# Output products of six heads as seven block products instead of eight, with one product copied by ScalarE into a second PSUM bank

## The chip, the cores and the metric

The kernel runs on one core of one Trainium2 chip. The metric is device time in microseconds (us) of one execution, the median of three runs. Five engines work side by side, each through its own instructions in order: PE (matrix products, with PEld for its weight loads), DVE (VectorE), ACT (ScalarE), POOL (GpSimd) and SP, which here only issues DMAs. They meet through semaphores. Matrix products are written to PSUM, which has eight banks of 128 partitions x 512 float32.

## The reference

A trunk of two layers is applied with the same weights to two groups of 512 tokens of width 1024. Each layer is `x = x + mixer(rms_norm(x))`. Layer 0 mixes by differential attention, layer 1 by retention in both directions; both have 8 heads of width 256 (`D_INNER` = 2048), a gate, and one output projection of 2048 x 1024:

```
o = rms_norm(o, subln_g, SUBLN_EPS) * (1.0 - lambda_init)     # layer 1: without the factor
o = o.reshape(B, S, D_INNER) * jax.nn.silu(gate)
return o @ w_out
```

A final RMS norm closes the trunk. What the change touches is `o @ w_out`: each head's 512 x 256 output times its 256 x 1024 rows of `w_out`, added to x.

## The kernel before, in words

Everything is float32 to the caller. A product of two float32 operands is done in three passes on operands split into a high and a low part (`PASSES`): high x high, high x low, low x high. `hi_of` (an ACT copy that rounds, line 481) makes the high part and `lo_of` (a DVE subtraction, line 484) the low one, so that every operand that is made costs both engines one instruction.

The program has four stages in time: projections of layer 0 (to about 620 us), attention with its output products (to about 1030), projections of layer 1 (to about 1480), and retention with its output products (to the end). The projections already use block products in seven multiplications (`P1` to `P7`, classes `Unit`, `Duo`, `WideDuo`); the output products do not.

Attention goes by `tiles` (head h, group g, 128 tokens t), two per turn of the loop: `scores`, `row_max`, `exps`, `combine`, `transp`, and after each second tile `av`, whose result `weigh` multiplies by the gate (`og`, line 1191) and splits into `oT`, and squares for the norm (lines 1195 and 1196). `weighed` gets the norm's factor `rr` (transposes on PE, sums on ACT, a power on POOL, line 1211). Retention goes by `blocks` (h, g), with `scores_both`, `states`, `av2` (c = 0, 1: 256 tokens each), `weigh`, and `weighed_both` (POOL lines 1911 and 1912 make `rr`).

Output products are owed (`owe`) as steps in a list `todo` that `fill` takes from while later tiles are worked on. A step (`out_step`) is one block of 128 tokens x 512 columns: six matmuls of 512 columns (two halves e of the head's 256 rows x three passes) into one of three `pj` banks of PSUM (line 1279), and then one DVE instruction (`axpy`, line 1284) that multiplies the bank by `rr` and adds it to x in SBUF. For 256 tokens of one head that is 4 steps, 24 matmuls and 4 axpys. The head's weights are loaded as two pieces of 128 x 1024 and each is split at that width (`out_weights`).

The order of instructions on each engine isn't written by hand. `Plan` records operations with costs and dependences, lists them by due time, and `SHIFTS` moves the due times of some operations by seeded random amounts; PE may take an operation up to 24 places early (`WINDOW`). What comes out is fixed when the program is built.

## Time and profile before

| | us |
|---|---|
| median of 3 runs | 1782.05 (1781.91 to 1782.11) |
| the profiled execution, its own time | 1782.33 |
| its span from first to last instruction | 1780.2 |
| PE busy | 1769.7 |
| DVE busy | 1550.6 |
| ACT busy | 926.9 |
| POOL busy | 118.5 |

An engine's busy time is the time in which one of its instructions was under way. Instructions of one engine overlap at their ends, so the step from one start to the next is shorter than an instruction's own duration; the step is what an instruction costs an engine that has no gaps.

### The profile page before, as it was taken

What the parts mean: (1) busy time and instruction counts of PE and PEld (TensorE: products, weight loads), DVE (VectorE), ACT (ScalarE), POOL (GpSimd) and SP (SyncE); (2) the same over time, 40 slices, a digit from 0 to 9 for tenths busy, and PEclk for the clock granted to TensorE, in tenths of its full rate; (3) what the DMA queues carried; (4) which work ended last, traced back from release to release, by engine and by line L of the source; (5) the groups of instructions that cost most, each with busy time, mean ns of one, the idle gap of its engine ahead of it and who ended that gap; (6) DMA issues with size and microseconds to landing.
All of it is one profiled execution on the core that took longest, in us unless ns stands there. A gap on an engine that the chain in (4) does not pass through costs nothing.

```text
span 1780.2 us, 28644 instructions
## 1 busy us (share of the span) xinstructions
PE 1769.7 (99%) x10485; PEld 1565.0 (88%) x10485; DVE 1550.6 (87%) x2660; ACT 926.9 (52%) x1947; POOL 118.5 (7%) x256
## 2 busy tenths in 40 slices
PE   9999999999999999999999999999999999999998
PEld 7889988888998888888888888899889988988887
DVE  8979779999979888888888898887998797888887
ACT  8664434544544565455455876444544455444446
POOL 1000000000000011111111100000000001111114
PEclk9999999999999999999999999999999999999999
DMA  6345535555555695455453624464565579665562
GB/s 233 102 153 168 177 118 160 171 160 168 190 175 155 218 332 187 174 189 190 168 190 105 213 77 155 138 200 166 172 206 179 176 222 407 236 232 194 217 221 95
DMA packets 162819, 328.85 MB, mean 185 GB/s; under 512 B 12772, under 2 KB 76920, under 8 KB 162680
## 3 DMA queue, kind: packets, MB, share of 16 engines
q1 hardware_dynamic: 162352, 326.71, 54.6%
q8 instruction: 82, 1.34, 0.3%
q14 instruction: 57, 0.47, 0.1%
q10 hardware_dynamic: 328, 0.34, 0.1%
HBM read 209.55 MB, written 117.44 MB: 184 GB/s over the span
## 4 chain that ended last, share of the span: by engine, by line
PE 98%; ACT 1%; DMA 1%; DVE 0%; issue 0%; POOL 0%; SPq 0%; POOLq 0%; DVEq 0%; ACTq 0%
PE pj L756 21%; PE pj L1279 19%; PE sc L756 11%; PE pj L766 10%; PE o L756 6%; PE o L1607 5%; PE sc L1546 5%; PE sc L766 5%; PE o L905 3%; PE o L991 2%; PE o L1864 1%; PE tp L1843 1%; PE sc L1816 1%; PE sc L1864 1%; PE pj L1587 1%; PE tp L1587 1%
## 5 line engine op out<-in xcount | busy, mean ns | idle before, releaser
L1279 PE MATMUL pj<-ws,arena 128*128 128x512 f32 (+1 forms) x1334 | 344.8, 390 | 0.0
L1279 PEld LDWEIGHTS pj<-ws,arena 128*128 128x128 f32 x1334 | 247.7, 188 | 50.4
L756 PE MATMUL pj<-b,ws 128*128 128x512 f32 x1080 | 263.5, 390 | 0.0
L481 ACT CAST ws<-st 128x512 fp32r<-128x512 f32 x264 | 161.1, 622 | 162.3 <-PE sc L756 37.5
L756 PEld LDWEIGHTS pj<-b,ws 128*128 128x128 f32 x1080 | 200.0, 188 | 40.4 <-issue 0.3
L484 DVE TENSOR_TENSOR ws<-st,ws 128x512 fp32r<-128x512 f32 x264 | 178.3, 687 | 50.8 <-ACT ws L481 38.4
L1284 DVE SCALAR_TENSOR_TENSOR b<-pj,pad,b 128x512 f32<-128x512 f32 (+1 forms) x257 | 189.6, 745 | 29.8 <-PE pj L1279 16.9
L756 PE MATMUL sc<-arena,ws 128*128 128x512 f32 x768 | 186.0, 390 | 0.0
L756 PEld LDWEIGHTS sc<-arena,ws 128*128 128x128 f32 x768 | 142.7, 188 | 28.9
L756 PE MATMUL pj<-arena,ws 128*128 128x512 f32 x636 | 156.0, 390 | 0.0
L756 PEld LDWEIGHTS pj<-arena,ws 128*128 128x128 f32 x636 | 118.8, 188 | 24.6 <-DVE ws L484 0.2
L481 ACT CAST ws<-raw 128x512 fp32r<-128x512 f32 (+2 forms) x140 | 103.2, 741 | 63.4 <-PE o L905 15.5
L484 DVE TENSOR_TENSOR ws<-raw,ws 128x512 fp32r<-128x512 f32 (+2 forms) x135 | 109.2, 813 | 23.4 <-ACT ws L481 21.1
L1564 ACT ACTIVATE b<-sc,pad 128x512 f32<-128x512 f32 x128 | 87.5, 691 | 74.3 <-DVE pad L1554 74.1
L766 PE MATMUL pj<-ws,b 128*128 128x256 f32 x960 | 116.1, 275 | 0.0
L766 PEld LDWEIGHTS pj<-ws,b 128*128 128x128 f32 x960 | 112.5, 188 | 0.3
L756 PE MATMUL o<-arena,ws 128*128 128x512 f32 x456 | 108.3, 390 | 0.4 <-DVE b L544 0.4
L1546 PE MATMUL sc<-arena 128*128 128x512 f32 x384 | 101.8, 398 | 0.7 <-ACT b L1564 0.7
L809 ACT COPY c<-pj 128x512 f32<-128x512 f32 x96 | 56.3, 588 | 87.1 <-PE pj L756 64.2
L756 PEld LDWEIGHTS o<-arena,ws 128*128 128x128 f32 x456 | 85.3, 188 | 18.3 <-DVE b L544 0.6
L481 ACT CAST os<-e 128x512 fp32r<-128x512 f32 x88 | 54.8, 622 | 77.6 <-DVE e L817 29.2
L1607 PEld LDWEIGHTS o<-arena 128*128 128x128 f32 x768 | 93.0, 188 | 2.4
(307 smaller groups left out, 3233.8 us busy)
## 6 DMA issues: line engine op xcount, KB each, us to landing
qk<-os SPq DMA_DIRECT2D x192, 256.0 KB, 3.6
arena<-qk SPq DMA_DIRECT2D x96, 512.0 KB, 7.0
v<-os SPq DMA_DIRECT2D x64, 512.0 KB, 3.6
arena<-v SPq DMA_DIRECT2D x64, 512.0 KB, 4.1
raw<-in_da_w_in_dram SPq DMA_DIRECT2D x51, 512.0 KB, 5.6
raw<-in_ret_w_in_dram SPq DMA_DIRECT2D x38, 512.0 KB, 5.0
os<-g SPq DMA_DIRECT2D x32, 512.0 KB, 7.2
g<-e SPq DMA_DIRECT2D x48, 256.0 KB, 4.2
```

The lines of the kernel that those rows point to most:

```text
L481: act(n, lambda: nc.scalar.copy(dst(), src()), r, w)
L484: dve(n, lambda: nc.vector.tensor_tensor(dst(), src(), hi().bitcast(F32), op=ALU.subtract), r, w)
L756: nc.tensor.matmul(ps.t, a[u][0]()[:, k, :], bt[k][:, v, :], start=(opens and k == 0 and i == 0), stop=(k == 3 and i == 2), skip_group_che ...
L766: nc.tensor.matmul(ps[:, (t % 2) * 256:(t % 2) * 256 + 256], bt[k][:, v, t * P:(t + 1) * P], a[u][0]()[:, k, :], start=(opens and t % 2 == ...
L809: act(S, lambda c=c, ps=ps: nc.scalar.copy(c.t, ps.t), [ps], [c])
L905: nc.tensor.matmul(ps[:, c0:c0 + 256], w[:, lo:lo + P], of(b, j), start=(start and j == 0 and i == 0), stop=(j == 1 and i == 2), skip_grou ...
L991: nc.tensor.matmul(ps[:, t * 256:t * 256 + 256], of(b, j, t), w[:, a, j], start=(start and t == 0 and j == 0 and i == 0), stop=(j == 1 and ...
L1279: nc.tensor.matmul(ps[:, here], o[a][:, e, t * P:(t + 1) * P], u[b][:, e, here], start=(m == 0), stop=(m == 5))
L1284: axpy(n, lambda half=half, here=here, ps=ps: nc.vector.scalar_tensor_tensor(half, ps[:, here], rr[:, t % 2:t % 2 + 1], half, op0=ALU.mult ...
L1546: nc.tensor.matmul(s.t, q[:, a, t * P:(t + 1) * P], k[:, b, :], start=(n == 0), stop=(n == 2))
L1564: act(840, lambda j=j, s=s, m=m: nc.scalar.activation(p[:, j, :], s.t, AF.Exp, bias=m.t, accum_out=sm[:, 2 * j + n:2 * j + n + 1]), [s, m] ...
L1607: nc.tensor.matmul(o[:, e * 256:(e + 1) * 256], v[b][:, j, e * P:(e + 1) * P], aT[a][:, j, :], start=(n == 0), stop=(n % 12 == 11), skip_g ...
```

## The change

For three heads of each layer (`FAST`: heads 2, 4, 6 of attention and 1, 3, 5 of retention), both groups and both halves c of the tokens, the product of a 256 x 256 block of o (2 x 2 blocks of 128) with the head's 256 x 1024 weights (2 x 2 blocks of 128 x 512) is done in seven block products instead of eight. Each is three matmuls. The seven share three `pj` banks: P1 goes to bank x, ACT copies x to bank y, P2 is added to y, P5 goes to z, P6, P7 and P4 are added to x and P3 to z. After P2, P5, P6, P7, P3 and P4 the bank is multiplied by `rr` and added to its quarter of x (`added`), six times in all.

Four sums of blocks of o are made per (h, g, c) on POOL (`block_sums`, 128 columns each) and split by ACT and DVE; the addition of the two halves of the squares moves from DVE to POOL for these heads. Per head four differences of weight blocks are made on POOL (512 columns each), and five operands of 512 columns are split (t1, t2, t3, t4, b22) beside one piece of 1024, where before two pieces of 1024 were. The first such product of a head issues the split of t4. `SHIFTS` has other and more entries (120 instead of 45).

```diff
+FAST = (2, 4, 6,), (1, 3, 5,)
...
 SHIFTS = (
-    (635.39, 16, 2, 0.05, 454008), (1473.67, 30, 2, 0.2, 912168), (1473.67, 8, 2, 0.2, 596270),
+    (1602.39, 8, 4, 0.5, 513480), (638.03, 16, 1, 0.5, 679689), (616.01, 30, 1, 1, 109496),
...
+        if dt == F32R and tag in ("e", "c", "m", "raw") or (tag, i) in rounded:
+            if rounded.get((tag, i), F32) != dt:
+                cnt[0] += 1
+                label = f"{tag}_{i}_{cnt[0]}"
+                places[tag, i] = pool.tile([P, size], dt, tag=f"{tag}{i}", name=label, bufs=1)
+            rounded[tag, i] = dt
...
+    def either(on, n, out, a, b, op, r, w):
+        plan.op(on, 0.2+0.0036*n if on == "POOL" else 0.07 + 0.00104 * n, lambda: (
+            nc.gpsimd if on == "POOL" else nc.vector).tensor_tensor(out(), a(), b(), op=op), r, w)
+    def block_sums(og, new):
+        x, hi, lo = st_t([P, S], "sums"), *(n(dt=F32R) for n in new)
+        a11, a21, a12, a22 = ((lambda k=k: og[:, k * P:(k + 1) * P]) for k in range(4))
+        s1, s2, s3, s4 = ((lambda k=k: x[:, k * P:(k + 1) * P]) for k in range(4))
+        for k, (o, a, b, fn, r) in enumerate((
+                (s1, a21, a22, ALU.add, [og]), (s2, s1, a11, ALU.subtract, [og, (x, 0)]),
+                (s3, a11, a21, ALU.subtract, [og]), (s4, a12, s2, ALU.subtract, [og, (x, 1)]))):
+            either('POOL', P, o, a, b, fn, r, [(x, k)])
+        hi_of(S, lambda: hi.t, lambda: x.t, [x], [hi])
+        lo_of(S, lambda: lo.t, lambda: x.t, lambda: hi.t, [x, hi], [lo])
+        return hi, lo
+    def weigh(y, sg, oT, c, scale=1.0, sq=None, sums=None, new=None):
         here = slice(c * 256, (c + 1) * 256)
-        og, sq = c_t("og"), sq or m_t("sq")
+        og, sq = e_t("og") if new and new[0] is m_t else c_t("og"), sq or m_t("sq")
         wide = lambda t: t.rearrange("p (e n) -> p e n", e=2)
         dve(S, lambda: nc.vector.tensor_tensor(wide(og.t), wide(y.t), sg[:, :, here], op=ALU.mult), [y, sg], [og])
         hi_of(S, lambda: oT[0][:, :, here], lambda: wide(og.t), [og], [(oT[0], c)])
         lo_of(S, lambda: oT[1][:, :, here], lambda: wide(og.t), lambda: oT[0][:, :, here], [og, (oT[0], c)],
               [(oT[1], c)])
         act(S, lambda: nc.scalar.activation(sq.t, y.t, AF.Square, scale=scale), [y], [sq])
-        dve(256, lambda: nc.vector.tensor_tensor(sq[:, 0:256], sq[:, 0:256], sq[:, 256:512], op=ALU.add), [sq], [sq])
+        if sums is not None:
+            sums.append(block_sums(og, new))
+        either("POOL" if sums is not None else "DVE", 256, lambda: sq[:, 0:256], lambda: sq[:, 0:256],
+               lambda: sq[:, 256:512], ALU.add, [sq], [sq])
         return sq
...
+    fastw, late = {}, {}
+    def fast_weights(w, h, t12):
+        r = [raw_t([P, 2, S]) for _ in range(2)]
+        for i in range(2):
+            src = w[h * 256:(h + 1) * 256, i * S:(i + 1) * S].rearrange("(e p) c -> p e c", p=P)
+            dma(lambda i=i: r[i].t, lambda src=src: src, [], [r[i]], 512)
+        hi, lo = ws_t([P, 2, S], 0, WS_BUFS), ws_t([P, 2, S], 0, WS_BUFS)
+        hi_of(1024, lambda: hi.t, lambda: r[0].t, [r[0]], [hi])
+        lo_of(1024, lambda: lo.t, lambda: r[0].t, lambda: hi.t, [r[0], hi], [lo])
+        out = fastw[h] = {}
+        for e, name in enumerate(("b11", "b21")):
+            out[name] = [((lambda t=t, e=e: t[:, e, :]), t) for t in (hi, lo)]
+        def parts(name, t, src, key):
+            a, b = (lambda: t[:, 0, :]), (lambda: t[:, 1, :])
+            hi_of(S, a, src, [key], [(t, 0)])
+            lo_of(S, b, src, a, [key, (t, 0)], [(t, 1)])
+            out[name] = [(a, (t, 0)), (b, (t, 1))]
+        b11, b21, b12, b22 = ((lambda i=i, e=e: r[i][:, e, :]) for i in range(2) for e in range(2))
+        x = [st_t([P, S], "ts") for _ in range(2)]
+        either('POOL', S, lambda: x[0].t, b12, b11, ALU.subtract, r, [x[0]])
+        parts("t1", t12[0](), lambda: x[0].t, x[0])
+        either('POOL', S, lambda: x[0].t, b22, lambda: x[0].t, ALU.subtract, [r[1], x[0]], [x[0]])
+        parts("t2", t12[1](), lambda: x[0].t, x[0])
+        either('POOL', S, lambda: x[1].t, b22, b12, ALU.subtract, [r[1]], [x[1]])
+        parts("t3", slot(30, [P, 2, S]), lambda: x[1].t, x[1])
+        either('POOL', S, b21, b21, lambda: x[0].t, ALU.subtract, [r[0], x[0]], [r[0]])
+        parts("b22", ws_t([P, 2, S], 0, WS_BUFS), b22, r[1])
+        late[h] = lambda: parts("t4", ws_t([P, 2, S], 0, WS_BUFS), b21, r[0])
+    def fast_owe(h, g, c, o, sums, rr):
+        banks = {}
+        tiles_ = [xN[g, 2 * c + t] for t in range(2)]
+        def a_of(e, t):
+            lo = (2 * c + t) * P
+            return [(lambda v=v: o[v][:, e, lo:lo + P]) for v in range(2)], [(o[v], c) for v in range(2)]
+        def s_of(k):
+            return [(lambda v=v: sums[v][:, k * P:(k + 1) * P]) for v in range(2)], list(sums)
+        of = dict(P1=(a_of(0, 0), "b11"), P2=(a_of(1, 0), "b21"), P3=(s_of(3), "b22"), P4=(a_of(1, 1), "t4"),
+                  P5=(s_of(0), "t1"), P6=(s_of(1), "t2"), P7=(s_of(2), "t3"))
+        def mult(name, at_, start=False):
+            (a, keys), v = of[name]
+            v = fastw[h][v]
+            if start:
+                banks[at_] = bank("pj")
+            ps = banks[at_]
+            def fn():
+                for i, (p, q) in enumerate(PASSES):
+                    nc.tensor.matmul(ps.t, a[p](), v[q][0](), start=(start and i == 0), stop=(i == 2),
+                                     skip_group_check=True)
+            pe(0.683, fn, keys + [v[0][1], v[1][1]], [ps])
+        def added(at_, t, i):
+            x, ps = tiles_[t], banks[at_]
+            half = x[:, i * S:(i + 1) * S]
+            axpy(S, lambda: nc.vector.scalar_tensor_tensor(
+                half, ps.t, rr[:, t:t + 1], half, op0=ALU.mult, op1=ALU.add), [ps, (x, i), rr], [(x, i)])
+        def first():
+            late.pop(h, lambda: None)()
+            mult("P1", "x", True)
+            x, y = banks["x"], bank("pj")
+            banks["y"] = y
+            act(S, lambda: nc.scalar.copy(y.t, x.t), [x], [y])
+            mult("P5", "z", True)
+            added("z", 1, 1)
+        def second():
+            mult("P2", "y")
+            added("y", 0, 0)
+            mult("P6", "x")
+            added("x", 0, 1)
+        def third():
+            mult("P7", "x")
+            added("x", 1, 1)
+        def fourth():
+            mult("P3", "z")
+            added("z", 0, 1)
+            mult("P4", "x")
+            added("x", 1, 0)
+        for part in (first, second, third, fourth):
+            owed[h, g] = owed.get((h, g), 0) + 1
+            def one(part=part):
+                owed[h, g] -= 1
+                part()
+            todo.append(one)
...
-        st[i].update(o=o, sq=weigh(o, sg[h, g], oT[h, g], t // 2, GUARD))
+        sums = st[i]['sums'] = [] if h in FAST[0] else None
+        st[i].update(o=o, sq=weigh(o, sg[h, g], oT[h, g], t // 2, GUARD, sums=sums, new=(e_t, e_t)))
...
+        if h in FAST[0]:
+            fast_owe(h, g, t // 2, oT[h, g], st[i]['sums'][0], rr)
+            return
...
+        if i < N and tiles[i][1:] == (0, 0) and tiles[i][0] in FAST[0]:
+            fast_weights(wo1, tiles[i][0], (lambda: slot(28, [P, 2, S]), lambda: slot(29, [P, 2, S])))
...
-        mid = m_t("mid")
-        mid2 = m_t("mid")
+        mid = e_t("mid")
+        mid2 = e_t("mid")
...
-        sqs[b, c] = weigh(y, sg[b], oT[h, g], c, sq=st_t([P, S], "sq"))
+        fast[b, c] = [] if h in FAST[1] else None
+        sqs[b, c] = weigh(y, sg[b], oT[h, g], c, sq=st_t([P, S], "sq"), sums=fast[b, c],
+                          new=None if fast[b, c] is None else (m_t, c_t))
...
+            if h in FAST[1]:
+                fast_owe(h, g, c, oT[h, g], fast[b, c][0], rr)
+                continue
...
+            if blocks[b][1] == 0 and blocks[b][0] in FAST[1]:
+                fast_weights(wo2, blocks[b][0], [lambda: raw_t([P, 2, S], 4, F32R)] * 2)
```

On PE, in retention, output products of head 3 and group g = 0. Before, two steps of six matmuls follow each other, each with a bank of its own (ws and both are weights, arena is o):

```order
L1279 MATMUL pj_1_357<-ws_2_80,arena_75 128x512
L1279 MATMUL pj_1_357<-ws_3_82,arena_75 128x512
L1279 MATMUL pj_1_357<-ws_2_80,arena_75 128x512 x2
L1279 MATMUL pj_1_357<-ws_3_82,arena_75 128x512
L1279 MATMUL pj_1_357<-ws_2_80,arena_75 128x512
L1279 MATMUL pj_2_406<-ws_4_84,arena_75 128x512
L1279 MATMUL pj_2_406<-both_183_14639,arena_75 128x512
L1279 MATMUL pj_2_406<-ws_4_84,arena_75 128x512 x2
L1279 MATMUL pj_2_406<-both_183_14639,arena_75 128x512
L1279 MATMUL pj_2_406<-ws_4_84,arena_75 128x512
```

After, at the same place (raw and b are weight operands t1, t2 and t3, m and c the split sums; pj_0 is bank y, pj_1 is z, pj_2 is x):

```order
L1406 MATMUL pj_0_294<-ws_2_80,arena_75 128x512
L1406 MATMUL pj_0_294<-ws_3_82,arena_75 128x512
L1406 MATMUL pj_0_294<-ws_2_80,arena_75 128x512
L1406 MATMUL pj_2_396<-raw_3_224_14697,m_3_210_14187 128x512 x2
L1406 MATMUL pj_2_396<-raw_3_224_14697,c_1_227_14918 128x512
L1406 MATMUL pj_1_355<-ws_4_84,m_3_210_14187 128x512 x2
L1406 MATMUL pj_1_355<-ws_4_84,c_1_227_14918 128x512
L2062 MATMUL tp_0_303<-ident_0_244,st_2_494 128x128 x2
L2062 MATMUL tp_0_303<-ident_0_244,st_0_467 128x128 x2
L1406 MATMUL pj_2_396<-b_152_14640,m_3_210_14187 128x512 x2
L1406 MATMUL pj_2_396<-b_152_14640,c_1_227_14918 128x512
```

The bank that was opened once for six matmuls is now written, read by DVE and written again, with other products of three matmuls and a pair of transposes between.

On DVE, in the same stretch. Before, one axpy (L1284) per bank stands between the instructions of the next block (st: squares, e: attention or retention outputs):

```order
L1196 TENSOR_TENSOR st_2_679<-st_2_679 128x256
L1883 TENSOR_TENSOR e_4_623<-sc_0_252,e_4_623 128x512
L1284 SCALAR_TENSOR_TENSOR b_127_236<-pj_1_357,pad_2_81,b_127_236 128x512
L484 TENSOR_TENSOR arena_75<-c_2_526,arena_75 128x2x256
L1284 SCALAR_TENSOR_TENSOR b_127_236<-pj_2_406,pad_2_81,b_127_236 128x512
L1196 TENSOR_TENSOR st_3_718<-st_3_718 128x256
L1191 TENSOR_TENSOR c_3_590<-e_4_623,os_2_598 128x512
L1284 SCALAR_TENSOR_TENSOR b_128_237<-pj_0_294,pad_2_81,b_128_237 128x512
L484 TENSOR_TENSOR ws_0_76<-raw_0_266,ws_6_88 128x1024
L1284 SCALAR_TENSOR_TENSOR b_128_237<-pj_1_357,pad_2_81,b_128_237 128x512
```

After, axpys of one 256-token block (L1413), with two splits of o (L516) and a product with the gate (L1241) among them:

```order
L516 TENSOR_TENSOR arena_75<-e_2_194_9703,arena_75 128x2x256
L1241 TENSOR_TENSOR e_4_190_9554<-e_3_196_9798,os_2_614 128x512
L1413 SCALAR_TENSOR_TENSOR b_137_237<-pj_1_355,pad_2_81,b_137_237 128x512
L1413 SCALAR_TENSOR_TENSOR b_136_236<-pj_0_294,pad_2_81,b_136_236 128x512
L1413 SCALAR_TENSOR_TENSOR b_136_236<-pj_2_396,pad_2_81,b_136_236 128x512
L516 TENSOR_TENSOR arena_75<-e_4_190_9554,arena_75 128x2x256
L1413 SCALAR_TENSOR_TENSOR b_136_236<-pj_1_355,pad_2_81,b_136_236 128x512
L1413 SCALAR_TENSOR_TENSOR b_137_237<-pj_2_396,pad_2_81,b_137_237 128x512
```

Three banks come round sooner, and pj_2 (x) is read at two places of these eight rows.

## Rows read from the trace of the kernel before

**Rows 1.** The page: busy us, tenths in 40 slices, last chain.

```profile
PE 1769.7 (99%) x10485; PEld 1565.0 (88%) x10485; DVE 1550.6 (87%) x2660; ACT 926.9 (52%) x1947; POOL 118.5 (7%) x256
...
PE   9999999999999999999999999999999999999998
...
PE 98%; ACT 1%; DMA 1%; DVE 0%; issue 0%; POOL 0%; SPq 0%; POOLq 0%; DVEq 0%; ACTq 0%
```

**Rows 2.** Windows: stretch, length, busy us by engine, clock, DMA.

```profile
280.00:440.00 160.00, 160.00 (x811) 136.59 (x810) 159.77 (x282) 74.22 (x131) 0.00 (x0) 1.00 0.57 163
...
1600.81:1637.44 36.63, 36.63 (x225) 32.64 (x225) 31.47 (x54) 15.62 (x42) 4.72 (x8) 1.00 0.57 215
...
804.00:852.16 48.16, 48.16 (x282) 42.45 (x281) 40.86 (x70) 23.93 (x66) 6.96 (x20) 1.00 0.47 176
```

**Rows 3.** Chain of waits in retention: start, us, engine and line, count.

```profile
1559.84 3.18 PE pj L1279 x14
...
1570.37 1.42 PE sc L1816 x12
```

**Rows 4.** Timeline of DVE in retention: start, us, instruction, [idle before, releaser].

```profile
1563.77 0.75 DVE L1284 SCALAR_TENSOR_TENSOR b<-pj,pad,b 128x512 f32<-128x512 f32 x1
1564.43 0.69 DVE L1191 TENSOR_TENSOR c<-e,os 128x512 f32<-128x512 f32 x1
1566.02 0.75 DVE L1284 SCALAR_TENSOR_TENSOR b<-pj,pad,b 128x512 f32<-128x512 f32 x1 [0.90 <-POOL pad L1912]
...
1570.87 0.43 DVE L484 TENSOR_TENSOR b<-tp,b 128x256 fp32r<-128x256 f32 x1 [1.13 <-ACT b L481]
...
1577.18 0.68 DVE L1191 TENSOR_TENSOR c<-e,os 128x512 f32<-128x512 f32 x1
1577.78 0.75 DVE L1284 SCALAR_TENSOR_TENSOR b<-pj,pad,b 128x512 f32<-128x512 f32 x1
...
1598.07 0.42 DVE L1196 TENSOR_TENSOR st<-st 128x256 f32<-128x256 f32 x1
1598.40 1.22 DVE L484 TENSOR_TENSOR both<-raw,ws 128x1024 fp32r<-128x1024 f32 x1
1599.53 1.41 DVE L1284 SCALAR_TENSOR_TENSOR b<-pj,pad,b 128x512 f32<-128x512 f32 x2
...
1601.05 0.69 DVE L1191 TENSOR_TENSOR c<-e,os 128x512 f32<-128x512 f32 x1
```

**Rows 5.** Groups by line: ACT copies; xcount, busy us, mean ns, idle.

```profile
L809 ACT COPY c<-pj 128x512 f32<-128x512 f32 x96 | 56.3, 588 | 87.1 <-PE pj L756 64.2 <-PE pj L766 22.1 <-DVE os L484 0.6
```

**Rows 6.** Groups by line, POOL.

```profile
L1912 POOL TENSOR_TENSOR pad<-pad,pad 128x2 f32<-128x2 f32 x26 | 20.9, 804 | 2.2
...
L1931 POOL TENSOR_TENSOR e<-b,cos 128x512 f32<-128x512 f32 x7 | 9.4, 1342 | 0.0
...
L1579 POOL TENSOR_TENSOR pad<-pad 128x2 f32<-128x2 f32 x32 | 6.3, 196 | 603.3 <-DVE pad L1573 603.3
```

**Rows 7.** Timeline of POOL in retention.

```profile
1601.04 0.78 POOL L1911 TENSOR_SCALAR pad<-pad 128x2 f32<-128x2 f32 x1 [16.23 <-ACT tp L1908]
...
1602.58 0.22 POOL L1911 TENSOR_SCALAR pad<-pad 128x2 f32<-128x2 f32 x1
```

**Rows 8.** DMA issues: KB each, median us from issue to landing.

```profile
raw<-in_ret_w_out_dram SPq DMA_DIRECT2D x16, 512.0 KB, 8.9
```

**Rows 9.** Groups of DVE in two heads, 1564.17 to 1637.44.

```profile
L484 DVE TENSOR_TENSOR arena<-e,arena 128x512 fp32r<-128x512 f32 x8 | 5.5, 687 | 0.4
L1191 DVE TENSOR_TENSOR c<-e,os 128x512 f32<-128x512 f32 x8 | 5.5, 686 | 0.0
L484 DVE TENSOR_TENSOR arena<-c,arena 128x512 fp32r<-128x512 f32 x8 | 5.5, 683 | 0.0
...
L484 DVE TENSOR_TENSOR ws<-raw,ws 128x1024 fp32r<-128x1024 f32 x3 | 3.6, 1217 | 0.0
...
L1196 DVE TENSOR_TENSOR st<-st 128x256 f32<-128x256 f32 x8 | 3.3, 418 | 0.0
```

More of the change, by code (lines that the diff above doesn't have):

```diff
@@ L310, in trunk_kernel @@
     SIZE = dict(raw=1024, st=512, c=512, e=512, m=512, os=1024)
-    places = {}
+    places, rounded = {}, {}
     cnt = [0]
@@ L324, in view @@
                 places[tag, i] = pool.tile([P, size], F32, tag=f"{tag}{i}", name=f"{tag}_{i}", bufs=1)
+        if dt == F32R and tag in ("e", "c", "m", "raw") or (tag, i) in rounded:
[4 more added lines that the diff above has]
+            rounded[tag, i] = dt
         t = places[tag, i][0:shape[0], 0:n]
-        if dt != F32:
+        if dt != F32 and (tag, i) not in rounded:
             t = t.bitcast(dt)
```

19 lines of the change are left out of this document (9 added, 10 removed), and 51 rows, old and new, of the table SHIFTS.

## The prediction

> **What bounds the kernel now.** I read the page first [rows 1]: PE is busy 1769.7 of 1780.2 us, its digit is 9 in 39 of 40 slices, and 98% of the chain that ended last is PE. So the kernel takes the time of its matrix products, and a product that goes is worth its full step until another engine becomes late. The next one is DVE, 87% busy over the span. Then I read windows, because a share over the whole span hides the stages [rows 2]: one head takes 36.63 us in retention, of which DVE is busy 31.47 and idle 5.16; one head takes 48.16 us in attention, of which DVE is busy 40.86 and idle 7.30. PE has no idle time in either. In the projections from 280 to 440 us DVE is busy 159.77 of 160 us and PE still 160.00, so a full DVE does not stop PE by itself, if its work lies ready ahead of time.
>
> **What a step costs.** PE: 14 products of 512 columns take 3.18 us, 0.227 each; 12 of 256 take 1.42 us, 0.118 each [rows 3]. DVE, from start to next start [rows 4]: an axpy 0.66 (1563.77 to 1564.43), 512 columns from SBUF 0.60 (1577.18 to 1577.78), 256 columns 0.33, 1024 columns 1.13 (1598.40 to 1599.53).
>
> **PE, removed.** 6 heads x 2 groups x 2 halves = 24 blocks of 256 tokens. Each had 8 x 3 = 24 matmuls and now has 21. The new order has 504 of them where 576 stood, and no other matmul more or fewer: 72 x 0.227 = **-16.3 us**, 2.7 per head. The DMAs are as many as before, with the same bytes, and SP has the same number of instructions.
>
> **DVE, added.** Per block: six axpys instead of four (+1.32), one split of the sums (+0.60), and the addition of squares gone to POOL (-0.33): +1.59. Per head: four blocks, 6.4, and the weights, five splits of 512 columns for one of 1024, 5 x 0.60 - 1.13 = +1.9; together 8.2 us. Over six heads 49.5 us. PE time falls by 2.7 per head while DVE work grows by 8.2. In retention a head of the new kind wants 36.63 - 5.16 + 8.2 = 39.7 us of DVE in 33.9 us of PE, in attention 49.1 in 45.4, if nothing of it runs beside a neighbouring head. Spread evenly over it and one old-style neighbour, retention wants 71.2 of DVE in 70.5 of PE, attention 90.0 in 93.6. So attention fits and retention is at its limit.
>
> To see how far the program spreads it I summed the steps above along the new order between marks that both engines have. In attention (marks: the row maxima) the output products of a head run beside the scores of the next one, and the three heavy stretches want 45.4, 44.2 and 39.1 us of DVE against 44.8, 44.8 and 38.9 of PE; inside them the worst 17.4 us of PE hold 20.8 us of DVE. In retention (marks: the scores), blocks 3 to 11 want 153.2 us of DVE against 149.6 of PE; in the old order it was 138.4 against 163.3.
>
> **Retention, lost again.** At least 3.6 us, the excess just named, as DVE can't work ahead of the products it reads. To that come DVE's own waits. In the old kernel each block of 18.3 us has two that matter, 0.90 us for POOL's norm and 1.13 us for ACT [rows 4]. If all nine blocks kept them, 9 x 2.03 = 18.3 more; if DVE ran as in the window from 280 to 440, nothing. Now another axpy or split stands in order at these places, so I take the value near the full window, 0.2 per block: 3.6 + 1.8 = **+5.4**, bounds 0 (old slack takes the excess) and 21.9.
>
> **Attention, lost again.** Bounds 0 and 3 x 3.4 (the worst excess, once per heavy stretch) = 10.2. The stretches before each have 6 us of DVE to spare, but only work that is ready can use it; I take 0.7 each, **+2**.
>
> **The banks.** x is written by P1, P6, P7 and P4 and read after each: ACT's copy, then three axpys, each of which must end before PE may write x again. The copy is like the copies out of PSUM at 0.59 us [rows 5]; P5 and often other products lie over it. Between P6 and P7 the order shows P3 and two transposes, some 0.9 to 1.1 us, over an axpy of 0.75 us and two semaphores: covered if DVE is free, and late by one step of 0.66 if it is not. Bounds 0 and 24 x 0.66 = 15.8; since the axpys stand in order right where they fall due I take **+1**, beside the waits already counted.
>
> **ACT and POOL.** ACT gains 24 copies and 54 splits less 6 wide ones, some 40 us, in stages where it is busy under half of the time [rows 2]: nothing. POOL gains 144 instructions. A 512-column one takes 1.34 us, a product of 128 x 2 takes 0.20 [rows 6]; by a line through the two, 128 columns are 0.48 and 256 are 0.77, all together 24 x (4 x 0.48 + 0.77 + 1.34), some 97 us over the two stages, where POOL is busy 4.7 of 36.6 and 7.0 of 48.2. What waits for it is the norm: rr now stands behind them in POOL's order. I take 0, bounds 0 and the 12 of the second rival below.
>
> When DVE works beside POOL both can lose. POOL's scaling of two columns takes 0.22 us alone and 0.78 when it starts at 1601.04 beside a DVE product of two SBUF tiles (1601.05 to 1601.74) [rows 4, 7]. The Trainium skill has a rule for it (SBUF — State Buffer, "Who interferes with whom"): a DVE instruction with two SBUF inputs and a POOL instruction that reads SBUF exclude each other for a whole instruction, and the first one wins. The row agrees for POOL as the loser; no row shows DVE losing, since the 512-column POOL work of the old kernel stands at its end.
>
> **Sum.** -16.3 + 5.4 + 2 + 1 = -7.9. The profiled execution took 1782.33 us (span 1780.2 and 2.1 around it), 0.3 over the median, so 1774.4 by the profile and **1774** beside the median of 1782.05.
>
> **The rivals.**
> - *Nearly all is kept*, 1767. For it: PE at 160.00 with DVE at 159.77 of 160, and the evenly spread sums of attention. Against it: the excess of 3.6 us in retention is arithmetic, and it leaves no room for a wait.
> - *All but the range of measurement is lost again, in POOL's queue*, 1782. Three weight differences of 1.34 us stand together in POOL's order, and they need w_out's load (8.9 us from issue to landing [rows 8]); the norm behind them comes 4 us later, and the axpys of up to three banks wait for rr. The banks give back 2 us: (4 - 2) x 6 heads = 12, of which I count a third as time in which DVE is waited for anyway: 1774 + 8 = 1782. For it: DVE's wait of 0.90 us for L1912. Against it: a head's weights may be made one head ahead.
> - *DVE sets the pace of the heavy heads*, slower. If work isn't spread, three heads in retention take 39.7 instead of 36.63 and three in attention 49.1 instead of 48.16: +9.2 +2.8 = +12, 1794. The point from which it decides: DVE's excess and waits above 16.3 us, 2.7 per head. By half of it spread, 1788. For it: the sum of 71.2 in 70.5. Against it: the order's own 3.6.
> - *DVE stands behind POOL*, 1786. In two heads of retention DVE spends 23.4 of 73.3 us, 32%, on instructions with two SBUF inputs [rows 9]; if each POOL instruction that meets one held it for half of its own length, 97 x 0.32 x 0.5 = 15 us of DVE would be lost, and some 12 of it where DVE has no slack. For it: POOL is held in the same way (0.78 for 0.22). Against it: no row shows DVE held. It is what the skill's rule above would do with POOL as the first one.
> - *The change doesn't remove what it says*: the order shows the 72 matmuls gone, so I give it nothing.
>
> **How the numbers follow.** A measurement of this kernel tells 0.2% or 3.6 us from no change: 1778.5 to 1785.6. The forecast (own range 1769 to 1778.5) has 0.53, nearly all kept 0.18, POOL's queue 0.11, DVE's pace 0.11, DVE behind POOL 0.07. Faster 0.53 + 0.18 = 0.71; POOL's queue and a share of the two last give 0.14 for the same; slower 0.15. The range goes from 1767 to 1785: below it and above it lie about 0.05 and 0.15.
>
> **What will show it.** Right: 10404 products on PE, its busy time down by 14 to 17 us against before; PE idle in small pieces of 0.1 to 0.7 us between the new products, released by DVE (line of `added`), more in retention than in attention; DVE busy over 95% in both. A head of retention of the new kind some 35 us, not 33.9. For POOL's queue: DVE's longest waits for L2072 or L1264, several us each. For DVE behind POOL: DVE instructions with two SBUF inputs longer than 0.69 us, or starting late, beside the new POOL rows. The forecast is wrong if PE is busy in windows of heavy heads as before (nearly all kept), or if DVE is full and PE idle for more than 3 us a head.

## The result, and the profile after

The changed kernel takes **1787.47 us** (1785.87 to 1789.19, 6 runs) against 1781.98 of the kernel before beside it: 1.0032 of it, 95% interval 1.0019 to 1.0045. It is slower by 5.5 us; 1774 was forecast, with a range from 1767 to 1785. The profiled execution took 1789.19 us, 1.7 over the median, with a span of 1787.4.

The page after, its busy line and its last chain, against [rows 1]:

```profile
PE 1765.6 (99%) x10413; PEld 1549.9 (87%) x10413; DVE 1607.8 (90%) x2731; ACT 962.9 (54%) x2020; POOL 240.2 (13%) x400
...
PE 91%; DVE 5%; DMA 1%; ACT 1%; issue 1%; POOL 1%; SPq 0%; POOLq 0%; DVEq 0%; ACTq 0%
```

72 products are gone, as the change says, but PE's busy time fell by 4 us and not by 16. A product's end is modelled, so small stalls count as busy; the chain tells more: DVE, ACT, POOL and DMA now stand in it with 8%, before with 2%. DVE's busy time grew by 57.2 us, of which 49.5 had been worked out.

Windows of the length of a heavy head: two in attention and two in retention, against [rows 2]:

```profile
840.00:888.00 48.00, 47.34 (x274) 39.92 (x273) 45.86 (x79) 29.87 (x79) 16.52 (x32) 1.00 0.56 204
936.00:984.00 48.00, 47.80 (x278) 40.06 (x276) 46.22 (x80) 28.39 (x76) 15.11 (x32) 1.00 0.28 103
1490.00:1526.00 36.00, 34.82 (x219) 31.02 (x218) 34.32 (x55) 16.86 (x45) 11.77 (x13) 1.00 0.90 351
1526.00:1562.00 36.00, 35.32 (x218) 30.32 (x217) 35.95 (x63) 20.53 (x56) 17.30 (x30) 1.00 0.73 260
```

DVE is at 95 to 100% and PE at 97 to 99.6%. To see what PE lost I took the time from each product's start to the next and summed what is more than 60 ns over its step [rows 3]. Before: 17.8 us in the whole program, 5.4 of it in attention and 1.4 in retention. After: 38.7, with 14.9 and 13.5. These 21 us, and some 2.5 in smaller pieces, are what stands against the 16.3: the span grew by 7.2.

By stage: the first product that only retention has starts here, before and after:

```profile
1473.93 0.86 PE L1797 MATMUL tp<-arena 128*128 128x256 f32 x6
```

```profile
1475.17 0.86 PE L1955 MATMUL tp<-arena 128*128 128x256 f32 x6
```

Each stage lost half of the 72 products, 8.2 us. Up to this mark the program became 1.2 us longer, so attention lost 9.4; from here to the end of the span it takes 312.2 us for 306.3, so retention lost 14.1.

Who released PE's longer waits, as the view of waits gives them; total us, times, longest. Attention (620 to 1040), then retention (1475 to 1745):

```profile
PE sc L1698 <- ACT b L1716: 1.9, 5, 0.8
PE sc L1594 <- ACT b L497: 1.6, 1, 1.6
PE pj L1739 <- DVE b L1413: 1.0, 1, 1.0
```

```profile
PE pj L1332 <- DVE b L1337: 3.3, 3, 2.0
PE pj L1406 <- DVE b L1337: 1.2, 2, 1.1
PE sc L1974 <- DMA arena<-qk: 1.1, 2, 1.0
PE pj L1406 <- DVE b L1413: 1.0, 3, 0.4
```

The kernel before had 1.1 us of such waits in attention and none in retention. In retention DVE's axpys come late. In attention the largest are of another kind: scores that wait for exponentials on ACT, and the norm at the end of the stage.

**DVE is held by POOL.** DVE and then POOL at 1509, where the weight differences of a head are made (start, us, instruction):

```profile
1509.59 1.78 DVE L1241 TENSOR_TENSOR c<-e,os 128x512 f32<-128x512 f32 x1
1511.30 1.78 DVE L516 TENSOR_TENSOR ws<-raw,ws 128x512 fp32r<-128x512 f32 x1
1513.00 0.74 DVE L1337 SCALAR_TENSOR_TENSOR b<-pj,pad,b 128x512 f32<-128x512 f32 x1
```

```profile
1509.27 1.55 POOL L1219 TENSOR_TENSOR st<-raw,raw 128x512 f32<-128x512 f32 x1
1510.79 1.75 POOL L1219 TENSOR_TENSOR st<-raw 128x512 f32<-128x512 f32 x1
```

The product that takes 0.69 us [rows 9] takes 1.78 here: it started while POOL's difference was under way, and it ends 0.55 us after the difference does. The split after it fares the same with the next one. Together 22 DVE instructions are over 0.25 us longer than the median of their operation and shape, 12.4 us in all: 21 beside one of the new POOL instructions, and one at 1780.91 beside a POOL product that the kernel before has as well. Before there was none by that measure. (The 14 us in the expectations below are an earlier count of the same.) The axpys from 1513.00 on come late, and PE waits for the second of them:

```profile
1514.45 0.74 PE L1332 MATMUL pj<-ws,arena 128*128 128x512 f32 x2 [1.18 <-DVE b L1337]
```

**POOL is held by DVE, and the orders hook into one another.** The chain that led to the largest stall (start, us, what):

```profile
1585.22 0.61 DVE raw L516
1585.83 0.07 issue
1585.90 4.03 POOL st L1219
1589.92 0.02 issue
1589.94 0.63 ACT raw L513
1590.57 0.02 issue
1590.59 0.04 DVE raw L516
1590.63 0.57 issue
1591.20 0.75 DVE b L1337
1591.96 0.04 issue
1592.00 2.05 PE pj L1332 x4
```

A weight difference of 1.285 us at its shortest took 4.0, from 1585.90 on. DVE had four instructions with two SBUF inputs one behind the other in that time:

```profile
1585.74 0.68 DVE L516 TENSOR_TENSOR arena<-c,arena 128x512 fp32r<-128x512 f32 x1
1586.34 1.82 DVE L516 TENSOR_TENSOR ws<-raw,ws 128x1024 fp32r<-128x1024 f32 x2
1588.08 0.68 DVE L516 TENSOR_TENSOR b<-st,b 128x512 fp32r<-128x512 f32 x1
```

The difference ends 1.16 us after the last of them. ACT and DVE waited for it to split it, and the axpy for which PE's bank waited stood behind that split on DVE.

### The profile page after: what moved, and what is told of

Its sections match the earlier page's. It is cut to its first block, busy times and chain, and to the rows that moved or that the text cites. A ratio compares the mean times of both kernels' runs of the same rounds, so it can differ in the third digit from the quotient of the medians.

```text
span 1787.4 us, 28770 instructions
## 1 busy us (share of the span) xinstructions
PE 1765.6 (99%) x10413; PEld 1549.9 (87%) x10413; DVE 1607.8 (90%) x2731; ACT 962.9 (54%) x2020; POOL 240.2 (13%) x400
## 3 DMA queue, kind: packets, MB, share of 16 engines
q8 instruction: 82, 1.34, 0.3%
## 4 chain that ended last, share of the span: by engine, by line
PE 91%; DVE 5%; DMA 1%; ACT 1%; issue 1%; POOL 1%; SPq 0%; POOLq 0%; DVEq 0%; ACTq 0%
PE pj L788 22%; PE sc L788 11%; PE pj L1332 10%; PE pj L798 10%; PE o L788 6%; PE sc L798 5%; PE pj L1406 5%; PE o L1759 5%; PE sc L1698 4%; PE o L937 3%; PE o L1023 2%; PE o L2022 1%; DVE b L1413 1%; DMA arena<-qk 1%; PE sc L1974 1%; DVE b L1337 1%
## 5 line engine op out<-in xcount | busy, mean ns | idle before, releaser
L1332 PE MATMUL pj<-ws,arena 128*128 128x512 f32 x854 | 220.3, 392 | 3.3 <-DVE b L1337 3.3
L516 DVE TENSOR_TENSOR ws<-st,ws 128x512 fp32r<-128x512 f32 x264 | 178.1, 686 | 47.7 <-ACT ws L513 29.7
L1332 PEld LDWEIGHTS pj<-ws,arena 128*128 128x128 f32 x854 | 158.7, 189 | 36.4 <-DVE b L1337 4.4
L516 DVE TENSOR_TENSOR ws<-raw,ws 128x512 fp32r<-128x512 f32 (+2 forms) x141 | 113.6, 810 | 24.0 <-ACT ws L513 20.8
L1337 DVE SCALAR_TENSOR_TENSOR b<-pj,pad,b 128x512 f32<-128x512 f32 (+1 forms) x161 | 118.0, 740 | 14.4 <-PE pj L1332 10.8
L1413 DVE SCALAR_TENSOR_TENSOR b<-pj,pad,b 128x512 f32<-128x512 f32 x144 | 103.2, 743 | 1.5 <-POOL pad L2072 0.6
```

The costliest lines, as they stand in the source:

```text
L516: dve(n, lambda: nc.vector.tensor_tensor(dst(), src(), hi().bitcast(F32), op=ALU.subtract), r, w)
L1332: nc.tensor.matmul(ps[:, here], o[a][:, e, t * P:(t + 1) * P], u[b][:, e, here], start=(m == 0), stop=(m == 5))
L1337: axpy(n, lambda half=half, here=here, ps=ps: nc.vector.scalar_tensor_tensor(half, ps[:, here], rr[:, t % 2:t % 2 + 1], half, op0=ALU.mult ...
L1413: axpy(S, lambda: nc.vector.scalar_tensor_tensor(half, ps.t, rr[:, t:t + 1], half, op0=ALU.mult, op1=ALU.add), [ps, (x, i), rr], [(x, i)])
```

## The experiments

Times are medians; the ratio is to runs of the kernel before on the same chip (1781.96 to 1782.17). The ladder down from the changed kernel (e6_diff_quarters and e14_diff_set are variants of the differences, not steps that follow from one another):

| run | what is left of the change | us | ratio (95%) |
|---|---|---|---|
| changed kernel | all | 1787.5 | 1.0032 (1.0019 to 1.0045) |
| e5_diff_unread | all, weight differences not waited for | 1785.9 | 1.0022 (1.0012 to 1.0031) |
| e6_diff_quarters | all, differences in four pieces | 1785.3 | 1.0017 (1.0008 to 1.0027) |
| e14_diff_set | fills in place of the differences, not waited for | 1782.1 | 1.0000 (0.9991 to 1.0010) |
| e2_diff_tiny | differences on 2 columns | 1781.3 | 0.9998 (0.9988 to 1.0007) |
| e1_pool_tiny | no POOL work to speak of | 1780.0 | 0.9991 (0.9982 to 1.0000) |
| e4_lo_tiny | POOL's work, no DVE splits | 1779.5 | 0.9987 (0.9977 to 0.9996) |
| e7_prep_tiny | no POOL work, no splits, no wait for differences | 1778.3 | 0.9981 (0.9972 to 0.9990) |
| e8_bare | and four axpys, no wait for the copy | 1775.8 | 0.9965 (0.9952 to 0.9978) |
| e13_bare_act | and no split of the sums on ACT | 1775.7 | 0.9967 (0.9955 to 0.9979) |
| e9_old_less | the 72 products fewer, old order | 1765.8 | 0.9909 (0.9894 to 0.9923) |

**POOL's work.** Every instruction stays in its place, but POOL's work on 2 columns; then the weight differences alone.

```diff
-            nc.gpsimd if on == "POOL" else nc.vector).tensor_tensor(out(), a(), b(), op=op), r, w)
+            nc.gpsimd if on == "POOL" else nc.vector).tensor_tensor(
+                *((t()[:, 0:2] if on == "POOL" else t()) for t in (out, a, b)), op=op), r, w)
...
+                *((t()[:, 0:2] if n == S else t()) for t in (out, a, b)), op=op), r, w)
```

> The changed kernel with every instruction in its place, but the 144 new POOL instructions (sums of blocks of o, differences of weights, additions of squares) work on 2 columns instead of 128, 256 or 512; the rest of their columns is left out. POOL loses some 95 us of work, DVE none. Load theory (DVE's 49.5 us of added work makes the loss of 21 us in PE's steps, POOL nothing): 1787, within 2. Lock theory (POOL and DVE instructions with two SBUF inputs exclude each other; 14.0 us of DVE is stretched and POOL's differences take up to 4 us): no DVE instruction over 0.8 us of those with two SBUF inputs, and the time falls by 8 to 14, to 1773 to 1779. Queue theory (the norm's rr and the weight operands come late behind the 512-column differences in POOL's order): falls too, by 4 to 10, and this run alone does not tell it from the lock.

> As the run before, but only the 24 weight differences of 512 columns work on 2 columns; the 96 sums of 128 columns and the 24 additions of squares are whole. Load theory: 1787, within 2. Queue theory: nearly all that the run before gains comes from these 24, so within 2 of it. Lock theory by time of exclusion: the 24 differences hold 24 x 1.3 = 31 of the 95 us of POOL work, so about a third to a half of the gain of the run before, 1782 to 1785.

1780.0 and 1781.3. No DVE instruction is stretched in the first, 2.5 us in the second. The load theory alone is out: it expected 1787 twice. The lock theory (DVE and POOL hold each other) missed its ranges by about 1 us each time, and the queue theory (results come late in POOL's order) fits both times, so these two runs don't tell the hold from the queue. Of POOL's 7.5 us the 24 differences make 6.1.

**Is it the wait, the queue, or the hold?** First nothing reads the differences; then each is cut in four; then POOL fills tiles in their place.

```diff
+            src = raw or src
...
-        parts("t1", t12[0](), lambda: x[0].t, x[0])
+        parts("t1", t12[0](), lambda: x[0].t, x[0], b12)
```

> The changed kernel with the 24 weight differences whole and in their place on POOL, but nothing reads them: the splits of t1, t2, t3 and t4 take the raw weights, and the fourth difference goes to a spare tile, so no operand waits for POOL's 512-column work. Shrinking these 24 to 2 columns was worth 6.1 us (1787.5 to 1781.3). If it is the wait of ACT's and DVE's splits for late differences: 1781 to 1783. If it is the exclusion (DVE held by 24 instructions of 1.3 us), or the norm that stands behind them on POOL: 1785 to 1788, and DVE instructions with two SBUF inputs are still stretched to 1.6 to 1.8 us.

```diff
+            for q in range(4):
+                at = slice(q * P, (q + 1) * P)
+                nc.gpsimd.tensor_tensor(out()[:, at], a()[:, at], b()[:, at], op=op)
```

> The changed kernel with each weight difference of 512 columns issued as four of 128 columns in the same place of POOL's order. POOL spends more on it, 4 x 0.46 = 1.84 us against 1.285, but no instruction is longer than 0.46 us alone. Lock theory with the length of an instruction as the price: DVE instructions that meet one are held at most 0.5 us instead of up to 1.1, so DVE's stretched total of 14 us falls to 6 or less and the time to 1782 to 1785. Queue theory: the differences and the norm behind them come later, 24 x 0.55 = 13 us more POOL time, 1787 to 1792.

```diff
+            for _ in range(2):
+                nc.gpsimd.memset(out(), 1.0)
```

> As the run in which nothing reads the weight differences (1785.9), but POOL fills the same 512-column tile twice with a constant in place of each subtraction, so its queue is held for about as long and it reads no SBUF. If the norm that is late behind them is the price: 1784 to 1787. If DVE held by POOL is the price: DVE's stretched total falls from 11 to about 2.5 us and the time to 1781 to 1782.5, as with differences of 2 columns. Should the fills be much shorter than 1.3 us, only the first outcome would tell.

1785.9: the wait for the differences is worth 1.6 us, no more than the runs spread. 1785.3: DVE's stretched total fell from 12.4 to 4.4, as the hold expects, and the time by 2.1, just short of what it expects (1785) and no more than the runs spread, while POOL's own time for the differences rose: the queue theory expected 1787 to 1792 from that, and is out as the main cause. DVE there, at the same place:

```profile
1507.73 0.95 DVE L1245 TENSOR_TENSOR c<-e,os 128x512 f32<-128x512 f32 x1
1508.61 0.94 DVE L516 TENSOR_TENSOR ws<-raw,ws 128x512 fp32r<-128x512 f32 x1
```

1782.1: with fills the stretched total is 2.4, and the time 3.9 below that of the run that differs in nothing else. DVE and POOL there:

```profile
1507.25 0.69 DVE L1245 TENSOR_TENSOR c<-e,os 128x512 f32<-128x512 f32 x1
1507.86 0.69 DVE L517 TENSOR_TENSOR ws<-raw,ws 128x512 fp32r<-128x512 f32 x1
1508.74 1.41 DVE L1341 SCALAR_TENSOR_TENSOR b<-pj,pad,b 128x512 f32<-128x512 f32 x2 [0.19 <-POOL st L1221]
```

```profile
1506.91 2.62 POOL L1221 MEMSET st<- 128x512 f32 x5
```

The two DVE instructions that took 1.78 take 0.69, beside a POOL that is as busy. A pair of fills takes 1.05 us against 1.3, so a part of the 3.9 may still be the shorter queue. It is a small part: these whole fills cost only 0.7 us against e2_diff_tiny (1781.3), where POOL has next to nothing at the same places. The bulk is the hold, of either engine by the other.

**The same work as load on DVE.** All of POOL's new work, then the differences alone, go to DVE.

```diff
-            nc.gpsimd if on == "POOL" else nc.vector).tensor_tensor(out(), a(), b(), op=op), r, w)
+            nc.vector).tensor_tensor(out(), a(), b(), op=op), r, w)
...
+            nc.gpsimd if on == "POOL" and n < S else nc.vector).tensor_tensor(out(), a(), b(), op=op), r, w)
```

> The changed kernel with the 144 new POOL instructions given to DVE in the same place of the order, whole: DVE gets 96 x 0.20 + 24 x 0.33 + 24 x 0.60 = 41.5 us more, and POOL has none of them, so nothing excludes anything. Load theory: DVE becomes the pace of the six heavy heads; 41.5 us more where it has no slack left, so 1787 + 25 to 41 = 1812 to 1828. Lock theory: the 14 us of stretched DVE and the late POOL results go, the load comes: 1787 + 10 to 25 = 1797 to 1812. Queue theory: the same direction as the lock, 1800 to 1815.

> The changed kernel whole, with the 24 weight differences done by DVE in the same place of the order, and the sums and additions of squares on POOL. DVE gets 24 x 0.60 = 14.4 us more, and loses about 10 us of being held. All 144 on DVE cost 20.3 us for 41.5 us of work, so by load 7.0 us for these, measured from 1787.5: 1793 to 1796. If what is given back by the hold (up to 4.6 us) comes on top of that as a gain of its own: 1787 to 1791.

1807.8 (1.0147, 1.0132 to 1.0162) and 1792.5 (1.0056, 1.0041 to 1.0071). So POOL is the better place for it: 41.5 us more on DVE cost 20.3, and 14.4 us cost 5.0, between the two expectations. A third to a half of what DVE gets is time, net of the hold that leaves with POOL's work; measured from 1780.0, where POOL's work costs next to nothing, the 41.5 us cost 27.8.

**DVE's splits**, on 2 columns, with POOL's work whole; then with POOL's work gone too.

```diff
-            lo_of(S, b, src, a, [key, (t, 0)], [(t, 1)])
-            out[name] = [(a, (t, 0)), (b, (t, 1))]
+            lo_few(S, b, src, a, [key, (t, 0)], [(t, 1)])
+            out[name] = [(a, (t, 0)), (a, (t, 1))]
```

> The changed kernel with every instruction in its place, but 54 of DVE's added splits (24 of sums, 30 of weight operands) work on 2 columns of 512; the products read the high part twice in their place. DVE loses 54 x 0.5 = 27 us of work, all of it in instructions with two SBUF inputs; POOL's work is whole. Load theory: more than half of the loss goes, 1770 to 1777. Lock theory: the splits are a third of what POOL can exclude, so a third of the 21 us, 1779 to 1783. Queue theory: POOL's queue is as long as before, 1783 to 1788.

> The three shortenings at once: new POOL instructions on 2 columns, nothing waits for the weight differences, and the 54 added DVE splits on 2 columns (the products read the high part twice). What is left of the change is the 72 products fewer, the six axpys and the copy per block, ACT's splits, and the new order. If the preparation of operands is all that costs: the loss of 21 us over the products' 16.3 nearly goes, 1766 to 1770. If the new products' banks and axpys, or the new order, cost as much: POOL's 7.5 and the splits' 7.9 us overlap, 1775 to 1779.

1779.5 and 1778.3. Without the splits 7.9 us go; without POOL's work 7.5; without both 9.2. The two are not added but meet: 27 us of splits, with the wait for the differences, cost 1.7 us when POOL does next to nothing (1780.0 against 1778.3), and 7.9 when it works. In e4_lo_tiny DVE is stretched as much as ever (12.6 us): a held DVE costs little once it has room again (at most the 1.2 us between 1779.5 and 1778.3).

**What is left with no added work**: two of six axpys on 2 columns and P2's bank begun afresh; then ACT's splits of the sums as well.

```diff
-            act(S, lambda: nc.scalar.copy(y.t, x.t), [x], [y])
+            act(S, lambda: nc.scalar.copy(junk.t, x[:, 0:2]), [x], [y])
...
-            added("x", 1, 1)
+            added("x", 1, 1, 2)
```

> As the run before, and besides two of the six axpys of each block (after P6 and after P7) work on 2 columns, and P2 starts its bank afresh, so that ACT's copy (2 columns into a spare tile) holds nobody. What is left is the 72 products fewer in the new order, with DVE's axpys as many as before. Banks and axpys as the cause of what is left: down to 1766 to 1769. The new order as the cause (the scores and transposes that wait in attention, the boundary stall of 1.8 us at 1017): within 2 of the run before.

```diff
-        hi_of(S, lambda: hi.t, lambda: x.t, [x], [hi])
+        act(S, lambda: nc.scalar.copy(hi[:, 0:2], x[:, 0:2]), [x], [hi])
```

> As the bare version, and ACT's 24 splits of the sums work on 2 columns too; the products with sums read another part of the head's output in their place, so that no product waits for a sum. ACT's added work falls from some 30 to 16 us, and 24 waits of PE on ACT go. If ACT's added work makes scores and transposes late in attention: 1769 to 1773. If the new order does: 1774.5 to 1776.5, with the stall of 1.8 us at the end of attention and those of the scores where they were.

1775.8 and 1775.7. Axpys and copy are worth 2.5 us; ACT's splits nothing. DVE has 1549.4 us of work in e8_bare, no more than before, and still 10 us of the 16.3 are lost. PE's waits in e8_bare, attention and then retention:

```profile
PE sc L1602 <- ACT b L497: 1.6, 1, 1.6
PE sc L1706 <- ACT pad L1429: 0.5, 1, 0.5
PE pj L1747 <- DVE b L1420: 0.4, 1, 0.4
```

```profile
PE sc L1982 <- DMA arena<-qk: 1.8, 3, 1.4
PE pj L793 <- DVE e L854: 0.4, 1, 0.4
PE tp L2070 <- DVE st L1223: 0.3, 1, 0.3
```

The 1.6 us at the end of attention stand there as in the changed kernel, and a load of q and k is late: DVE's and POOL's amount of work can't be the reason, as it is gone. But the waits that the view names are 5.2 us against 1.1 before, so they make some 4 of the 10. PE's excess steps (27.9 us against 17.8) do add up to the 10; the rest of them is in pieces too short to be named.

**The old order**, with the products left out and nothing added; then with DVE's load added.

```diff
-                for e in range(2):
+                some = h in FAST[w is wo2] and t % 2 == i == 1
+                for e in range(1 if some else 2):
...
+                more = h in FAST[w is wo2] and (t % 2 == 1 or i == 1)
+                for _ in range(2 if more else 1):
+                    nc.vector.scalar_tensor_tensor(
```

> The kernel before, in its own order, with 72 products left out: in the same six heads one output step of every block of 256 tokens (its second column half for the odd tile) does three products instead of six. No operand, axpy, copy or POOL work is added, and DVE, ACT and POOL have what they had. If the 10 us that the bare version of the change still loses come from the new order: this keeps nearly all, 1782 - 16.3 = 1766 to 1768. If they come from engines that are late as soon as PE is shorter (row maxima and exponentials in attention, axpys in retention): it loses about as much as the bare version, 1773 to 1777.

> As the run before, and three of the four axpys of each of these 24 blocks are done twice: 72 more DVE instructions of 0.66 us, 47.5 us, about the change's 49.5, spread over the old order, and none on POOL. Load theory (DVE's added work costs by itself, wherever it stands): well above the run before, by 8 to 15 us. If DVE's slack takes it: within 3 us of the run before; then POOL's work and the new order are what the change pays for.

1765.8: the 72 products are worth 16.4 us, all of it. No other engine is late when PE is shorter. 1799.0 (1.0095, 1.0078 to 1.0112): 47.5 us of axpys in an order not made for them cost 33.2, well over the 8 to 15 that load theory expected. PE's waits in that run, attention and then retention:

```profile
PE pj L1592 <- DVE b L1581: 12.3, 12, 1.6
PE sc L1551 <- ACT b L1569: 0.7, 1, 0.7
PE o L757 <- DVE b L545: 0.4, 1, 0.4
```

```profile
PE tp L1907 <- DVE st L1197: 7.3, 6, 1.4
PE pj L1281 <- DVE b L1289: 4.9, 8, 0.9
PE pj L1281 <- DVE ws L485: 0.5, 1, 0.5
```

Softmax's own DVE steps (L1581) come behind the added axpys, twelve times. The new order spares most of this, and pays for it elsewhere.

**The order itself.** Both kernels and the bare version with the table of shifts emptied, and the bare version with the planner told its true costs.

```diff
-SHIFTS = (
-    (1602.39, 8, 4, 0.5, 513480), (638.03, 16, 1, 0.5, 679689), (616.01, 30, 1, 1, 109496),
...
+SHIFTS = ()
```

> The changed kernel whole, with the table that shifts due times emptied, so that its order is the planner's own. To be read against the next run, the kernel before with an empty table. If the change pays by itself and the new table is the worse fit: this one is 3 to 10 us faster than the next. If the change costs by itself: 3 to 8 us slower than the next, as with the tables.

> The kernel before with the table that shifts due times emptied. The table's moves are of 0.05 to 1 us each and stand where the order had stalls, so I expect the kernel to lose 3 to 15 us by it: 1785 to 1797. The old order without its table has about as many late operations as the new one with its table has left, if the order is what the bare version still pays for.

> The bare version (72 products fewer, added work of POOL, DVE's splits and two of six axpys on 2 columns, no wait for the copy) with the table of shifts emptied: the planner's own order, made as if the added work were there. The table was worth 11.2 us to the changed kernel, most of it against late DVE work that the bare version doesn't have, so 1775.8 plus 2 to 8: 1778 to 1784.

```diff
-        dve(n, lambda: nc.vector.tensor_tensor(dst()[:, 0:2], src()[:, 0:2], hi()[:, 0:2].bitcast(F32),
+        dve(2, lambda: nc.vector.tensor_tensor(dst()[:, 0:2], src()[:, 0:2], hi()[:, 0:2].bitcast(F32),
...
-            axpy(S, lambda: nc.vector.scalar_tensor_tensor(
+            axpy(n, lambda: nc.vector.scalar_tensor_tensor(
```

> The same instructions with the table emptied, and the planner told what they cost now: the shortened ones as short, no dependence on the weight differences. The old kernel without its table takes 1785.6, and 16.3 less is 1769.3. If the loss of the bare version comes from an order made for work that isn't there: 1769 to 1773. If it lies in the seven products themselves (three banks, sums that hang on one another, waits between products and axpys): as the run before, within 3.

| table emptied | us | with its table |
|---|---|---|
| kernel before | 1785.6 (ratio 1.0020, 1.0011 to 1.0029) | 1782.0 |
| changed kernel | 1798.7 (1.0094, 1.0079 to 1.0109) | 1787.5 |
| bare, planned as the changed kernel | 1785.4 (1.0017, 1.0008 to 1.0027) | 1775.8 |
| bare, planned with its own costs | 1778.2 (0.9979, 0.9970 to 0.9988) | - |

The new table isn't the worse fit: it gives 11.2 us, the old one 3.6, and without tables the change costs 13.1. Two programs with the same instructions, which differ in what the planner was told and in that the splits of weights no longer wait for POOL's 2 columns, are 7.2 us apart: that much the bare version pays, without a table, for an order that makes room for work which is not there. 1778.2 fits neither of the two expectations, which lay at 1769 to 1773 and near 1785: both causes hold in part. The other 8.9 (1778.2 against 1785.6 - 16.3 = 1769.3) stayed when the costs were true: they come with the seven products themselves, their banks, sums and loads, or with how well the planner can place them. That part was not taken further apart, and how the 10 us of the bare version with its table divide between order and products isn't shown.

**Fewer heads**, with the old table.

```diff
-FAST = (2, 4, 6,), (1, 3, 5,)
+FAST = (4,), (3,)
```

> The change in one head of attention (4) and one of retention (3) alone, with the old table of shifts: 24 products fewer, 5.4 us, and a third of all the added work. If the loss goes by heads, 21.8 / 6 = 3.6 each: 1782.0 - 5.4 + 7.3 = 1784. If it comes from heavy heads that stand close together and DVE's slack around a single one takes its 8.2 us: 1777 to 1780. An order that the old table no longer fits can cost up to 3.6 more (1785.6 without a table).

1787.0 (1.0028, 1.0017 to 1.0040): with 24 products fewer PE's excess steps are 27.2 us for 17.8. The loss by heads (1784) with nearly all that an unfitting table was allowed (3.6) would make this time. The run doesn't part the two, but slack around a single heavy head didn't make it faster than before (1777 to 1780 was expected of that). A third of the change costs nearly as much as the whole. Of the runs that compute the whole reference none is faster than the kernel before.

## Why the prediction was wrong

**What held.** The price of a product (16.3, measured 16.4), DVE's full windows in the heavy heads, the durations of the POOL instructions (estimated 0.48, 0.77 and 1.34; at their median 0.46, 0.74 and 1.55, the last at least 1.285). The copy and the banks: +1 was taken, and the copy's wait with two of the axpys makes 2.5. One sign was miscounted: 10485 - 72 is 10413 and not 10404, and 10413 products were recorded. The sign of being wrong that was named, DVE full and over 3 us lost on PE per head, came: (9.4 + 14.1) / 6 = 3.9.

**The step that failed first: "ACT and POOL ... I take 0".** POOL's new work costs 7.5 us. The mechanism was among the rivals, "DVE stands behind POOL", with a chance of 0.07 and "no row shows DVE held" against it. DVE lost 12.4 us by instructions stretched over 0.25 us where 15 were worked out, and the hold costs some 4 us of time by the fills in place of differences, where 12 were given to it; the rest is the wait for late differences (1.6 by e5_diff_unread), POOL's queue (0.7 by the fills) and the 128- and 256-column work (1.3 by e2_diff_tiny and e1_pool_tiny). So that rival's 1786, near the measured time, is luck, as is the 1788 of DVE's pace by half.

"No row shows DVE held" was also a misreading. POOL's 512-column work of the kernel before stands from 1752 on, mostly beside axpys, but one DVE instruction there reads two SBUF inputs. POOL and then DVE, before and after:

```profile
1773.04 1.27 POOL L1931 TENSOR_TENSOR e<-b,sin 128x512 f32<-128x512 f32 x1
1773.87 0.71 DVE L1305 SCALAR_TENSOR_TENSOR c<-b 128x256 f32<-128x256 f32 x1
```

```profile
1780.44 1.27 POOL L2094 TENSOR_TENSOR e<-b,sin 128x512 f32<-128x512 f32 x1
1780.91 1.08 DVE L1457 SCALAR_TENSOR_TENSOR c<-b 128x256 f32<-128x256 f32 x1
```

The same DVE instruction starts 0.83 us behind POOL's in one and 0.47 in the other, and ends 0.28 us after POOL's in both: in each it ran only when POOL was done. The Trainium skill has the rule (SBUF — State Buffer, "Who interferes with whom") that names both sides, and also that a POOL instruction which only writes SBUF does not contend. Both agree with the runs here: 1.78 us beside a difference, 0.69 beside a fill.

**The step that failed most: the sum had no term for the order.** "Attention, lost again ... +2" and "Retention, lost again ... +5.4" were DVE's sums against PE's along the new order, with the stalls taken to be DVE's excess. All that the stages lost came out as 9.4 and 14.1. Both lie inside the bounds that were given (10.2 and 21.9), but far above the values taken, and not by DVE alone: e8_bare, with DVE's work as before, loses 10. Late instructions of the new order that are not DVE's excess were left out: scores behind exponentials, the norm at the stage's end, loads of q and k. They are some 4 of the 10; whose the short pieces are stays open. From 1765.8 up to the changed kernel's 1787.5 there are 10.0 of order and structure of the seven products, 2.5 of axpys and copy, 1.7 of splits and the wait for weights with POOL at rest, and 7.5 of POOL beside them: 21.7.

**Load.** "If DVE ran as in the window from 280 to 440, nothing" was the lower end, and the value was taken near it. That window is in the projections. In the heavy heads 47.5 us of axpys cost 33.2 in the old order (e10_old_load), while the change's 27 us of splits cost 1.7 in the new one with POOL at rest: they differ in kind and in order, so the amount alone doesn't give the price. The rival "DVE sets the pace" had +12; with POOL at rest splits, axpys and copy together cost 4.2.

**POOL's queue**, the second rival, 0.11: the wait for late differences is 1.6 us and the queue behind fills 0.7, not the 8 that it was given.

## What to carry to other kernels

When a change gives work to an idle POOL, look at what DVE runs beside it: if DVE is full and reads two SBUF operands, each POOL instruction that reads SBUF can cost up to its own length on DVE and be starved by it in turn. Look for it in the trace before by instructions that are longer than others of their kind, single ones too. Price a saving on the bounding engine with a run that takes the work away and adds nothing (here 16.4 us, all kept), and the preparation with runs that keep every place and shrink one engine's part; what remains then is the order. In a program whose order is planned to within a microsecond, put a term for the new order into the sum: here order and structure of the new products took 10 of the 16 us.

## What the runs showed of the hardware

- DVE and POOL hold each other for whole instructions: 0.69 us became 1.78 beside a POOL subtraction of 1.55, and a POOL subtraction of 1.285 became 4.0 beside four DVE instructions. In all 20 traces the DVE instruction at the program's end that is shown above ends 0.28 us after POOL's, whether it started 0.47 or 0.84 us behind it (1.08 to 0.71 us long). DVE's axpys, with one operand from PSUM, were not held (three in 2.06 us from 1591.20, beside a difference from 1590.85), nor was any DVE instruction that met only fills.
- Cut into pieces of 128 columns POOL's subtractions hold DVE for 0.26 us at a time instead of 1.09 (0.95 against 1.78 for the same product).
- A stall of 1.97 us on PE was followed by a lower granted clock, 0.50 in the window from 1592.5 to 1594.5:

```profile
1592.50:1594.50 2.00, 2.00 (x6) 1.54 (x5) 1.09 (x3) 0.87 (x4) 0.81 (x2) 0.50 0.00 0
```

```profile
1592.00 2.91 PE L1332 MATMUL pj<-ws,arena 128*128 128x512 f32 x6 [1.97 <-DVE b L1337]
```

That is 1.2 GHz, the lower of the clock's two levels. Five of the six products behind the stall take 427 ns a step instead of 227: 1.0 us on top of it.
